# Where expert weights land, where a loop of spare blocks stands, and when two broadcast rows are loaded

## The chip, the cores and the metric

One core of a Trainium2 chip runs the whole program. The metric is the time of one execution in microseconds (us), taken on the device. The core has TensorE (PE), VectorE (DVE), ScalarE (ACT), GpSimd (POOL), and SyncE (SP), which does nothing here but start DMA transfers from its queue, in program order; POOL starts some as well. On-chip tiles lie in SBUF, sums of matmuls in PSUM.

## The reference

The program is two transformer blocks in float32 on 512 tokens of width 1024. Only the end of the second one matters here: a mixture of 32 experts, two for each token.

```python
x = layer_norm_2(alpha * x + (1.0 + gt1) * y, ln_g[l, 0], ln_b[l, 0])
h = x * (1.0 + sc2) + sh2
y = hier_moe(h, w_route_grp[l], w_route_exp[l], w_gate[l], w_up[l], w_down[l])
x = layer_norm_2(alpha * x + (1.0 + gt2) * y, ln_g[l, 1], ln_b[l, 1])
...
# in hier_moe, for the rows xb that were routed to expert e:
hb = jax.nn.silu(xb @ w_gate[e]) * (xb @ w_up[e])
return hb @ w_down[e]
```

Each expert has gate and up weights of 1024 x 512 and down weights of 512 x 1024, 6.29 MB together, 201 MB for all of them.

## The kernel before

The dense part (first block, then the second one's mixer) takes up the first 1520 us or so. After it the pools `pool` (left side of SBUF) and `wpool` (right side) are closed, and `ep1` and `ep2` take over their space; a tile there waits for the old tiles whose bytes it overlaps.

**Weights.** `ew` issues one load of 512 KB from SP's queue into a tile that `eraw` hands out: 128 partitions with 4096 bytes each. `eraw` goes round a ring of 22 such tiles, 12 in `ep1` and 10 in `ep2`. An expert takes twelve loads: four of gate (g), four of up (u), and four of down (d). Each load on SP's queue tells of its landing through one of eight semaphores in turn, and the load eight places further on waits for that one, so no more than eight are under way. In the first pass two loads go into a tile named `first` of the tag `xs` (the list `ex`), as a 23rd and 24th buffer. The program as built puts the `ep1` tiles 480 bytes and the `ep2` tiles 192 bytes past a multiple of 512.

**Compute.** The loop over `e` runs `gate_up` for expert e and, woven into it, `down` for expert e - 1 and one of the eight steps of `gather`, which picks the rows of the next four experts by matmuls with a one-hot matrix (`xg`, line 1751). Each expert has 64 rows. The results `y` go to DRAM (`y_d`) two experts at a time by a store on POOL's queue (line 1884).

**Overflow.** An expert with over 64 rows gets extra blocks. `overflow` runs them in a loop whose count is read from memory (`ovi`) on every engine; with these inputs the body isn't entered, as the trace shows 128 loads of each kind of weight and no more. The loop stands ahead of the expert with index `E_OV` = 8. Just ahead of it `eraw`'s count is set to 0, and the four loads of d of expert 7 and the eight of g and u of expert 8 are issued (`rawd`, `rawg`).

**Residual and last norm.** `residual` starts at index `E_RES` = 14: it loads two broadcast rows (`lg`, `lb`, 512 KB each once spread over partitions) into two tiles of the ring and scales `x_sb` on DVE (8 instructions). At index 28 (`NE - 4`) two more broadcast rows, `lg2` and `lb2`, are loaded into a tile of tag `xs` (lines 1845 and 1846).

**End.** After expert 31's loads, eight indirect loads on POOL's queue (line 1906) fetch each token's two result rows from `y_d` into tiles of the ring. ACT scales the pair of the last token block (line 1935) before POOL adds them (line 1936). A last layer norm follows, and eight stores.

The order of instructions on each engine comes from a scheduler that goes by the program's order and by when buffers come free.

Of the kernel before, what the change touches and what calls it, by code (L numbers as in the profile page):

```python
# [13 lines left out]
F32 = mybir.dt.float32  # L14
# [7 lines left out]
D = 1024  # L22
P = 128
# [26 lines left out]
def tile_model(ctx: ExitStack, tc: tile.TileContext, A: dict, out: bass.AP):  # L50
# [1377 lines left out]
    V.tensor_tensor(hgc, col["ln_g0"], sc2, ALU.mult)  # L1428

    pcol = lambda ap: ap.rearrange("o (q p j) -> p (o q) j", q=4, j=2)  # L1430
    pv = cst(32, "pv").rearrange("p (a q j) -> p a q j", a=4, j=2)
    for i, ap in enumerate((A["ln_g_2"][0, 0:1, :], A["ln_b_2"][0, 0:1, :], mod_row[:, 4 * D : 5 * D], mod_row[:, 3 * D : 4 * D])):
        SY.dma_start(pv[:, i], pcol(ap))
    pv = pv.rearrange("p a q j -> p a (q j)")
# [100 lines left out]
    halve_z(NT - 1)  # L1535

    panels.close()
    ep1 = ctx.enter_context(tc.tile_pool(name="ep1", bufs=1, side="right", reuse_waits="tile"))
    dense.close()
    ep2 = ctx.enter_context(tc.tile_pool(name="ep2", bufs=1, side="left", reuse_waits="tile"))  # L1540
    N1 = NRAW + 8
    N2 = 10
    nraw, ex = [0], []

    def eraw(loop=False):
        i = nraw[0] % (N1 + N2)
        if not loop and ex:
            if nraw[0] >= N1 + N2:
                return ex.pop(0)
        if loop:  # L1550
            i = N1
        else:
            nraw[0] += 1
        if i < N1:
            return ep1.tile([P, D], F32, tag="eraw", name=nm("eraw"), bufs=N1)
        return ep2.tile([P, D], F32, tag="eraw2", name=nm("eraw"), bufs=N2)
# [8 lines left out]
        return raw  # L1565

    wg, wu, wd = A["w_gate_2"][0], A["w_up_2"][0], A["w_down_2"][0]
    raws0 = [ew(w, 2, q) for q in range(4) for w in (wg[0], wu[0])]


    def ytile():
# [5 lines left out]
    def xtile():  # L1577
        return ep2.tile([P, ND * 256], F32, tag="xs", name=nm("xs"), bufs=2)

    first = xtile()  # L1580
    ex.extend(first[:, i * D : (i + 1) * D] for i in range(2))
    xs0 = xtile()
    scr = [etile("scr"), 0]
    oh0 = [ytile(), ytile()]
# [91 lines left out]
    def routing():  # L1676

        ge, gs, e2 = rt(4, "ge"), rt(1, "gs"), rt(1, "e2")
        tc.keep_in_program_order(V.tensor_tensor(ge, gl, bc(gm, 4), ALU.subtract))
        SC.activation(ge, ge, AF.Exp)  # L1680
        tc.keep_in_program_order(V.tensor_tensor(e2, m2, m1, ALU.subtract))
        SC.activation(e2, e2, AF.Exp)
        tc.keep_in_program_order(V.tensor_reduce(gs, ge, axis=AX.X, op=ALU.add))
        V.reciprocal(gs, gs)
        tc.keep_in_program_order(V.tensor_scalar(gate1, e2, 1.0, None, ALU.add))
        V.reciprocal(gate1, gate1)
        V.tensor_tensor(gate1, gate1, gs, ALU.mult)
# [24 lines left out]
        for j in range(2):  # L1712
            V.tensor_tensor(rj[j], rowt, E[j], ALU.mult)
            V.tensor_reduce(rowf[:, j, :], rj[j], axis=AX.X, op=ALU.add)
        V.tensor_copy(rows_i, rowf)

        ovf = cpool.tile([1, 16], F32, name="ovf")
        ovc = rs_(NOV * NE)[0:1].rearrange("p (b e) -> p b e", b=NOV)
        V.tensor_tensor(ovc, oe[0:1, :].rearrange("p (o e) -> p o e", o=1).to_broadcast([1, NOV, NE]),
                        iota[0:1, :NOV].rearrange("p (b o) -> p b o", o=1).to_broadcast([1, NOV, NE]), ALU.is_le)  # L1720
        V.tensor_reduce(ovf[:, 0:NOV], ovc, axis=AX.X, op=ALU.add)
        V.tensor_scalar(ovf[:, 0:NOV], ovf[:, 0:NOV], float(NE - 1), None, ALU.min)
        V.tensor_copy(ovf[:, 15:16], oe[0:1, NE - 1 : NE])
        V.tensor_copy(ovi, ovf)
        V.tensor_scalar(relv, rflat, -float(NE * CAP), None, ALU.add)
# [2 lines left out]
    rowf = cpool.tile([P, 2, NT], F32, name="rowf")  # L1728
    rflat = rowf.rearrange("p j t -> p (j t)")
    rows_i = cpool.tile([P, 2, NT], I32, name="rows_i")  # L1730
    ovi = cpool.tile([1, 16], I32, name="ovi")
    relv = cpool.tile([P, 8], F32, name="relv")

    gt2 = ep2.tile([P, S], F32, name="gt2")
# [22 lines left out]
                V.tensor_scalar(xs[:, c], pv, pg[:, c : c + 1], pb[:, c : c + 1], ALU.mult, ALU.add)  # L1757
            yield

    def gate_up(wg, wu, xs, res, raws=(), loop=False):  # L1760

        ps = mm("gu")
        for q in range(4):
            rw = raws[2 * q : 2 * q + 2] if raws else [ew(w, 2, q, loop) for w in (wg, wu)]
            for k in range(2):
                for m in range(2):
                    PE.matmul(ps[m * CAP : (m + 1) * CAP, :], lhsT=xs[0][:, 2 * q + k, xs[1], :], rhs=rw[m][:, k * S : (k + 1) * S],  # L1767
                              start=q == 0 and k == 0, stop=q == 3 and k == 1)
                if q < 3 or k == 0:
                    yield  # L1770
        g = etile("eg")
        SC.activation(g[CAP:, :], ps[:CAP, :], AF.Silu)  # L1772
        V.tensor_tensor(g[:CAP, :], ps[CAP:, :], g[CAP:, :], ALU.mult)  # L1773
        res.append(g)
        yield

    def down(wd, g, y, raws=(), loop=False, rg=None):

        ps = mm("hT")
        for c in range(4):  # L1780
# [4 lines left out]

        py = acc("py")
        for c in range(4):
            raw = raws[c] if raws else ew(wd, 1, c, loop)
            for half in range(2):
                PE.matmul(py[half * CAP : (half + 1) * CAP, :], lhsT=hT[:, c * CAP : (c + 1) * CAP], rhs=raw[:, half * S : (half + 1) * S],  # L1790
                          start=c == 0, stop=c == 3)
# [13 lines left out]
    def overflow():  # L1805

        n_ov = nc.values_load(ovi[0:1, 15:16], min_val=0, max_val=NOV)
        with tc.For_i(0, n_ov, 1) as ib:
            ei = nc.values_load(ovi[0:1, bass.ds(ib, 1)], engines=(mybir.EngineType.SP,), min_val=0, max_val=NE - 1)
            dyn = lambda w: w[bass.ds(ei, 1)].rearrange("o k n -> (o k) n")  # L1810
            xo, go = [], []
            run(gather(relv, 1, xo))
            run(gate_up(dyn(wg), dyn(wu), (xo[0], 0), go, loop=True))
            yo = ytile()
            run(down(dyn(wd), go[0], yo[:CAP, :], loop=True))
            SY.dma_start(y_d[bass.ds(ib * CAP + NE * CAP, CAP), :], yo[:CAP, :])
            V.tensor_scalar(relv, relv, -float(CAP), None, ALU.add)

    def residual():

        lg, lb = eraw(), eraw()
        SY.dma_start(lg, A["ln_g_2"][0, 0:1, :].partition_broadcast(P))
        SY.dma_start(lb, A["ln_b_2"][0, 0:1, :].partition_broadcast(P))
        for t in range(NT):
# [2 lines left out]
            V.scalar_tensor_tensor(x_sb[t], lb, ALPHA, x_sb[t], ALU.mult, ALU.add)  # L1827
            yield

    E_OV = 8  # L1830
    E_RES = 14
    xg, gx = [], []
    gx.append(gather(None, 4, xg, ov0))
    downs, done = [], []
    for e in range(NE):
# [4 lines left out]
        if e == NE - 4:  # L1840
# [29 lines left out]
        if e == E_OV:  # L1870

            nraw[0] = 0
            rawd = [ew(wd[e - 1], 1, c) for c in range(4)]
            rawg = [ew(w, 2, q) for q in range(4) for w in (wg[e], wu[e])]
            overflow()
            gx.append(gather(rel_cols((e // 4 + 1) * 4 * CAP), 4, xg))
        gu = gate_up(wg[e], wu[e], (xg[e // 4], e % 4), g, rawg)
        for i in range(8):
            next(gu)
            if i == 2 and e:  # L1880
                downs.append(down(wd[e - 1], gp, yp, rawd, rg=rgs[:, 0:1] if e == NE - 1 else None))
            downs = [d for d in downs if next(d, 1) is None]
            if i == 2 and e > 2 and e % 2:
                GP.dma_start(y_d[(e - 3) * CAP : (e - 1) * CAP, :], yd)
# [113 lines left out]
```

## Time and profile before

| what | value |
|---|---|
| time, median of 3 runs | 2114.64 us (2114.31 to 2116.75) |
| the profiled execution's own time | 2116.61 us |
| its span, first to last instruction | 2114.9 us |
| PE busy | 2000.5 us (95%) |
| DVE busy | 1239.6 us (59%) |
| ACT busy | 758.5 us (36%) |
| bytes moved by DMA | 377.05 MB |

Busy time is a share of the whole span, over stages with different limits; a matmul's end is modelled in it, so a busy PE need not be a PE at its peak. The stage of the experts, from about 1520 us on, has to be read from stretches of its own.

### The profile page before, as it was taken

The numbers are of one execution on the slowest core, as the hardware profiler recorded it, in microseconds if no ns is written. First come the engines' busy times: TensorE is split into PE (matmuls) and PEld (weight loads), VectorE is DVE, ScalarE is ACT, GpSimd is POOL, SyncE is SP. The second block draws the span as 40 slices with busy tenths as digits, with TensorE's granted clock in tenths as the row PEclk, the third lists the DMA queues.
The fourth block names the chain that finished last, engine by engine and source line by source line (L and its number), as shares of the span: only waits on it lengthen the run. The fifth ranks groups of instructions, "written<-read, shape, count | busy, mean of one in ns | idle before, by whom it ended". The sixth has DMA issues, their size and how long they took to land. (4 is left out here: it accounts for less than half of the span.)

```text
span 2114.9 us, 25924 instructions
## 1 busy us (share of the span) xinstructions
PE 2000.5 (95%) x9522; PEld 1399.0 (66%) x9522; DVE 1239.6 (59%) x2816; ACT 758.5 (36%) x1403; POOL 91.2 (4%) x117
## 2 busy tenths in 40 slices
PE   7999989999999999999989999999989899999893
PEld 6887668877877778887878877778744343333321
DVE  4898666687468667799998643535542223212216
ACT  4433873443233346754545324542311000000002
POOL 1000100000000010000000000010100000000003
PEclk9999999999999999999999999999989999999997
DMA  4343005366446345533133232143299899999993
GB/s 133 103 105 90 20 21 179 111 203 183 132 149 198 98 119 137 141 78 89 36 79 81 74 89 70 50 120 106 80 352 402 341 409 410 409 410 411 371 411 130
DMA packets 306341, 377.05 MB, mean 178 GB/s; under 512 B 45828, under 2 KB 225548, under 8 KB 306212
## 3 DMA queue, kind: packets, MB, share of 16 engines
q1 hardware_dynamic: 301748, 359.12, 50.7%
q0 software_dynamic: 4464, 16.25, 2.0%
q8 instruction: 76, 1.25, 0.2%
q14 instruction: 53, 0.43, 0.1%
HBM read 354.06 MB, written 21.26 MB: 177 GB/s over the span
## 5 line engine op out<-in xcount | busy, mean ns | idle before, releaser
L99 DVE TENSOR_TENSOR wl<-wraw,wh 128x1024 fp32r<-128x1024 f32 (+1 forms) x196 | 236.8, 1209 | 211.9 <-ACT wh L98 210.8
L98 ACT CAST wh<-wraw 128x1024 fp32r<-128x1024 f32 (+1 forms) x196 | 202.7, 1036 | 398.5 <-PE up L129 72.2
L1767 PE MATMUL gu<-eraw,xs 128*64 128x512 f32 x1016 | 319.8, 616 | 15.4 <-DMA eraw<-in_w_up_dram 8.5
L1767 PEld LDWEIGHTS gu<-eraw,xs 128*64 128x64 f32 x1016 | 82.7, 139 | 155.8 <-issue 102.3
L128 PE MATMUL pc<-hi,wh 128*128 128x512 f32 (+2 forms) x480 | 176.9, 374 | 0.6 <-ACT hi L98 0.4
L129 PE MATMUL pc<-lo,wh 128*128 128x512 f32 (+2 forms) x480 | 173.4, 364 | 0.5 <-DVE lo L99 0.5
L130 PE MATMUL pc<-hi,wl 128*128 128x512 f32 (+2 forms) x480 | 173.1, 363 | 0.0
L1790 PE MATMUL py<-eraw,ehT 128*64 128x512 f32 x512 | 160.5, 603 | 2.8 <-DVE ehT L1783 1.3
L1773 DVE TENSOR_TENSOR eg<-gu,eg 64x512 f32<-64x512 f32 x32 | 22.2, 693 | 236.5 <-ACT eg L1772 236.1
L128 PE MATMUL up<-hi,wh 128*128 128x512 f32 x328 | 130.9, 399 | 0.0
L129 PE MATMUL up<-lo,wh 128*128 128x512 f32 x328 | 129.7, 395 | 0.0
L130 PE MATMUL up<-hi,wl 128*128 128x512 f32 x328 | 129.7, 395 | 0.0
L1772 ACT ACTIVATE eg<-gu 64x512 f32<-64x512 f32 x32 | 18.8, 588 | 283.1 <-PE gu L1767 283.1
L130 PEld LDWEIGHTS pc<-hi,wl 128*128 128x128 f32 (+1 forms) x480 | 90.1, 188 | 12.4
L128 PEld LDWEIGHTS pc<-hi,wh 128*128 128x128 f32 (+1 forms) x480 | 90.0, 189 | 12.5 <-ACT hi L98 1.0
L129 PEld LDWEIGHTS pc<-lo,wh 128*128 128x128 f32 (+1 forms) x480 | 90.5, 189 | 11.4 <-DVE lo L99 0.7
L1790 PEld LDWEIGHTS py<-eraw,ehT 128*64 128x64 f32 x512 | 44.3, 138 | 72.6 <-issue 56.9
L449 DVE SCALAR_TENSOR_TENSOR u<-u,cols_dw 128x497 f32<-128x497 f32 (+14 forms) x120 | 84.8, 750 | 0.7
L1755 ACT ACTIVATE xs<-xg,pb,pg 128x256 f32<-128x256 f32 x32 | 18.0, 564 | 174.1 <-PE xg L1751 174.1
L1751 PEld LDWEIGHTS xg<-oh,zNh 128*128 128x128 f32 x224 | 42.6, 190 | 53.1 <-issue 40.6
L128 PEld LDWEIGHTS up<-hi,wh 128*128 128x128 f32 x328 | 61.6, 188 | 23.8 <-ACT wh L98 7.8
L1757 DVE TENSOR_SCALAR xs<-xg,pg,pb 128x256 f32<-128x256 f32 x32 | 17.4, 543 | 100.4 <-PE xg L1751 100.4
(627 smaller groups left out, 4388.9 us busy)
## 6 DMA issues: line engine op xcount, KB each, us to landing
eraw<-in_w_down_dram SPq DMA_DIRECT2D x128, 512.0 KB
eraw<-in_w_gate_dram SPq DMA_DIRECT2D x127, 512.0 KB
eraw<-in_w_up_dram SPq DMA_DIRECT2D x127, 512.0 KB
wraw<-in_w_in_dram SPq DMA_DIRECT2D x91, 512.0 KB
wada<-in_w_ada_dram SPq DMA_DIRECT2D x48, 512.0 KB
wraw<-in_w_ffn_up_dram SPq DMA_DIRECT2D x44, 512.0 KB
wraw<-in_w_ffn_down_dram SPq DMA_DIRECT2D x20, 512.0 KB
wraw<-in_w_out_dram SPq DMA_DIRECT2D x16, 512.0 KB
```

The costliest lines, as they stand in the source:

```text
L98: c = SC.copy(r(hi), src)
L99: (eng or V).tensor_tensor(r(lo), src, hi, ALU.subtract)
L128: PE.matmul(ps, lhsT=wh, rhs=xh, start=start, stop=False)
L129: PE.matmul(ps, lhsT=wh, rhs=xl, start=False, stop=False)
L130: PE.matmul(ps, lhsT=wl, rhs=xh, start=False, stop=stop)
L449: yield lambda j=j, lo=lo, hi=hi, s=s: V.scalar_tensor_tensor(a[:, lo:hi], u[:, lo + s : hi + s], dww[:, j * 4 + c : j * 4 + c + 1], a[:, ...
L1751: PE.matmul(ps[:, :n], lhsT=hN[t][s_][:, c * P : (c + 1) * P], rhs=r(ov[:, t, :]), start=t == 0 and s_ == 0, stop=t == NT - 1 and s_ == 1)
L1755: SC.activation(xs[:, c], pv, AF.Identity, scale=pg[:, c : c + 1], bias=pb[:, c : c + 1])
L1767: PE.matmul(ps[m * CAP : (m + 1) * CAP, :], lhsT=xs[0][:, 2 * q + k, xs[1], :], rhs=rw[m][:, k * S : (k + 1) * S], start=q == 0 and k == 0 ...
L1772: SC.activation(g[CAP:, :], ps[:CAP, :], AF.Silu)
L1773: V.tensor_tensor(g[:CAP, :], ps[CAP:, :], g[CAP:, :], ALU.mult)
L1790: PE.matmul(py[half * CAP : (half + 1) * CAP, :], lhsT=hT[:, c * CAP : (c + 1) * CAP], rhs=raw[:, half * S : (half + 1) * S], start=c == 0 ...
```

## The change

It does five things. The weight tiles come to lie at multiples of 512 bytes: small tiles (`pv`, `ovf`, `ovi`) leave `cpool`, and paddings of 480 and 64 bytes are put ahead of `ep1` and `ep2`. The `first` tile, and with it the 23rd and 24th buffer, is gone. `overflow` moves from index 8 to 16, with 11 loads issued ahead of it in the order of use and no reset of the ring. `residual` moves from index 14 to 18 and takes tiles of its own (tag `yhl`, which `yh` and `yl` use at the end). `lg2` and `lb2` are loaded at index 30, where they were at 28.

```diff
+    PAD_R = 120
...
-    pv = cst(32, "pv").rearrange("p (a q j) -> p a q j", a=4, j=2)
+    pv = small(32, "pv").rearrange("p (a q j) -> p a q j", a=4, j=2)
...
+    padr = ctx.enter_context(tc.tile_pool(name="padr", bufs=1, side="right"))
+    GP.memset(padr.tile([P, PAD_R], F32, name="padr"), 0.0)
     ep1 = ctx.enter_context(tc.tile_pool(name="ep1", bufs=1, side="right", reuse_waits="tile"))
     dense.close()
+    padl = ctx.enter_context(tc.tile_pool(name="padl", bufs=1, side="left"))
     ep2 = ctx.enter_context(tc.tile_pool(name="ep2", bufs=1, side="left", reuse_waits="tile"))
...
     def eraw(loop=False):
+        if loop:
+            return ep2.tile([P, D], F32, tag="yhl", name=nm("lraw"), bufs=2)
         i = nraw[0] % (N1 + N2)
-        if not loop and ex:
-            if nraw[0] >= N1 + N2:
-                return ex.pop(0)
-        if loop:
-            i = N1
-        else:
-            nraw[0] += 1
+        nraw[0] += 1
...
-    raws0 = [ew(w, 2, q) for q in range(4) for w in (wg[0], wu[0])]
+    early = {}
+
+    def ld(w, e, q):
+
+        if (w, e, q) in early:
+            return early.pop((w, e, q))
+        return ew({"g": wg, "u": wu, "d": wd}[w][e], 1 if w == "d" else 2, q)
+
+    def ahead(e, n):
+
+        for i in range(n):
+            x = "g0 u0 g1 u1 d0 g2 u2 d1 d2 g3 u3 d3".split()[i % 12]
+            k = (x[0], e + i // 12 - (x[0] == "d"), int(x[1]))
+            if k[1] >= 0:
+                early[k] = ld(*k)
+
+    ahead(0, 12)
...
-    first = xtile()
-    ex.extend(first[:, i * D : (i + 1) * D] for i in range(2))
...
-        ovf = cpool.tile([1, 16], F32, name="ovf")
+        ovf = small(16, "ovf")[0:1, :]
...
-    ovi = cpool.tile([1, 16], I32, name="ovi")
+    ovi = padl.tile([P, 16], I32, name="ovi")[0:1, :]
...
-        lg, lb = eraw(), eraw()
+        lg, lb = eraw(True), eraw(True)
...
-    E_OV = 8
-    E_RES = 14
+    E_OV = 16
+    E_RES = 18
...
-            SY.dma_start(lg2, A["ln_g_2"][0, 1:2, :].partition_broadcast(P))
-            SY.dma_start(lb2, A["ln_b_2"][0, 1:2, :].partition_broadcast(P))
...
+        if e == NE - 2:
+            SY.dma_start(lg2, A["ln_g_2"][0, 1:2, :].partition_broadcast(P))
+            SY.dma_start(lb2, A["ln_b_2"][0, 1:2, :].partition_broadcast(P))
...
         if e == E_OV:
-
-            nraw[0] = 0
-            rawd = [ew(wd[e - 1], 1, c) for c in range(4)]
-            rawg = [ew(w, 2, q) for q in range(4) for w in (wg[e], wu[e])]
+            ahead(e, 11)
             overflow()
...
-    yh = ep2.tile([P, D], F32, name="yh")
-    yl = ep2.tile([P, D], F32, name="yl")
+    yh, yl = (ep2.tile([P, D], F32, tag="yhl", name=nm("yhl"), bufs=2) for _ in range(2))
```

Three places in the order of instructions follow. The first is SP's queue just ahead of the loop, which begins with the load of `ovi`. Before, the first of these rows is the last of four loads of expert 7's down weights, and the rest are expert 8's gate and up weights:

```order
L1564 DMA eraw_14007<-in_w_down_dram 128x1024
L1562 DMA eraw_14009<-in_w_gate_dram 128x1024
L1562 DMA eraw_14011<-in_w_up_dram 128x1024
L1562 DMA eraw_14013<-in_w_gate_dram 128x1024
L1562 DMA eraw_14015<-in_w_up_dram 128x1024
L1562 DMA eraw_14017<-in_w_gate_dram 128x1024
L1562 DMA eraw_14019<-in_w_up_dram 128x1024
L1562 DMA eraw_14021<-in_w_gate_dram 128x1024
L1562 DMA eraw_14023<-in_w_up_dram 128x1024
L1807 TENSOR_LOAD ovi
L1808 COMPARE_AND_BRANCH
```

In the changed kernel the eleven rows ahead of the loop are loads of experts 15 (down) and 16 (gate, up):

```order
L1563 DMA eraw_14706<-in_w_gate_dram 128x1024
L1563 DMA eraw_14708<-in_w_up_dram 128x1024
L1563 DMA eraw_14710<-in_w_gate_dram 128x1024
L1563 DMA eraw_14712<-in_w_up_dram 128x1024
L1565 DMA eraw_14714<-in_w_down_dram 128x1024
L1563 DMA eraw_14716<-in_w_gate_dram 128x1024
L1563 DMA eraw_14718<-in_w_up_dram 128x1024
L1565 DMA eraw_14720<-in_w_down_dram 128x1024
L1565 DMA eraw_14722<-in_w_down_dram 128x1024
L1563 DMA eraw_14724<-in_w_gate_dram 128x1024
L1563 DMA eraw_14726<-in_w_up_dram 128x1024
L1822 TENSOR_LOAD ovi
```

The loop went from between experts 7 and 8 to between 15 and 16, and one load fewer stands ahead of it.

The second place is where the two broadcast rows stand on SP's queue, before between loads of expert 28:

```order
L1564 DMA eraw_15936<-in_w_down_dram 128x1024
L1562 DMA eraw_16002<-in_w_gate_dram 128x1024
L1845 DMA xs_15948<-in_ln_g_dram 128x1024
L1846 DMA xs_15948<-in_ln_b_dram 128x1024
L1562 DMA eraw_16004<-in_w_up_dram 128x1024
L1562 DMA eraw_16010<-in_w_gate_dram 128x1024
```

In the changed kernel they stand ahead of expert 30's loads:

```order
L1565 DMA eraw_16122<-in_w_down_dram 128x1024
L1875 DMA xs_15957<-in_ln_g_dram 128x1024
L1876 DMA xs_15957<-in_ln_b_dram 128x1024
L1563 DMA eraw_16137<-in_w_gate_dram 128x1024
L1563 DMA eraw_16139<-in_w_up_dram 128x1024
L1563 DMA eraw_16145<-in_w_gate_dram 128x1024
```

They moved behind some two experts' worth of weight loads.

The third is POOL's queue at the end, from the last store of results to the last indirect load. Before, two indirect loads of token block 2, two of block 3, the additions of block 3, and then blocks 0 and 1:

```order
L1884 DMA y_d<-ey_15947 128x1024
L1906 DMA eraw_16268<-y_d,rows_i 128x1024
L1906 DMA eraw_16270<-y_d,rows_i 128x1024
L1906 DMA eraw_16272<-y_d,rows_i 128x1024
L1906 DMA eraw_16274<-y_d,rows_i 128x1024
L1936 TENSOR_TENSOR eraw_16272<-eraw_16272,x_12644 128x1024
L1936 TENSOR_TENSOR x_12644<-eraw_16274,eraw_16272 128x1024
L1906 DMA eraw_16260<-y_d,rows_i 128x1024
```

In the changed kernel (block 3's tiles are `eraw_16281` and `eraw_16283`):

```order
L1896 DMA y_d<-ey_15956 128x1024
L1919 DMA eraw_16273<-y_d,rows_i 128x1024
L1919 DMA eraw_16275<-y_d,rows_i 128x1024
L1919 DMA eraw_16277<-y_d,rows_i 128x1024
L1919 DMA eraw_16279<-y_d,rows_i 128x1024
L1919 DMA eraw_16281<-y_d,rows_i 128x1024
L1919 DMA eraw_16283<-y_d,rows_i 128x1024
L1948 TENSOR_TENSOR eraw_16281<-eraw_16281,x_12644 128x1024
L1948 TENSOR_TENSOR x_12644<-eraw_16283,eraw_16281 128x1024
```

Block 1's pair now stands ahead of block 3's, since other tiles of the ring come free first.

## Rows read from the trace of the kernel before

**Rows 1.** The page: what the DMA engines moved, in 40 equal slices.

```profile
GB/s 133 103 105 90 20 21 179 111 203 183 132 149 198 98 119 137 141 78 89 36 79 81 74 89 70 50 120 106 80 352 402 341 409 410 409 410 411 371 411 130
```

**Rows 2.** Stretches of 20 us: engines' busy time, clock, DMA share, GB/s.

```profile
1560.00:1580.00 20.00, 20.00 (x99) 7.90 (x99) 4.85 (x15) 3.02 (x4) 0.00 (x0) 1.00 0.86 323
...
1660.00:1680.00 20.00, 14.68 (x62) 5.74 (x62) 7.27 (x17) 0.59 (x1) 0.53 (x1) 0.89 0.67 241
...
1760.00:1780.00 20.00, 20.00 (x93) 7.79 (x94) 8.78 (x17) 1.15 (x2) 0.00 (x0) 1.00 1.03 409
1780.00:1800.00 20.00, 15.66 (x67) 4.97 (x64) 9.32 (x11) 1.18 (x2) 0.53 (x1) 0.91 1.03 411
...
1980.00:2000.00 20.00, 14.26 (x80) 5.11 (x77) 5.75 (x17) 0.59 (x1) 0.00 (x0) 0.91 0.82 307
```

**Rows 3.** Waits of SP's queue, 1690 to 1960 us: us in total, times, longest.

```profile
SPq L1562 <- DMA eraw<-in_w_up_dram: 46.9, 49, 2.9
...
SPq L1562 <- PE gu L1767: 2.4, 10, 0.4
```

**Rows 4.** Timeline around the loop: start us, us, engine, line, operation, tile.

```profile
1659.69 0.33 SPq L1562 DMA_DIRECT2D eraw<-in_w_up_dram  x1
...
1670.28 0.33 SPq L1562 DMA_DIRECT2D eraw<-in_w_gate_dram  x1
...
1671.14 0.33 SPq L1562 DMA_DIRECT2D eraw<-in_w_up_dram  x1
...
1676.22 1.98 PE L1767 MATMUL gu<-eraw,xs 128*64 128x512 f32 x4 [5.12 <-SPq L1808]
...
1677.44 0.34 SPq L1562 DMA_DIRECT2D eraw<-in_w_gate_dram  x1
```

**Rows 5.** The instructions of line 1845: duration ns min/median/max, first and last start.

```profile
L1845 SPq EVENT_SEMAPHORE  x2: 17/4783/9549, 1979.4 to 1980.3; - x2
```

**Rows 6.** Timeline of ACT: the Silu that ends experts 6, 7, and 19 to 23.

```profile
1658.83 0.59 ACT L1772 ACTIVATE eg<-gu 64x512 f32<-64x512 f32 x1 [9.45 <-PE gu L1767]
1670.28 0.59 ACT L1772 ACTIVATE eg<-gu 64x512 f32<-64x512 f32 x1 [10.86 <-PE gu L1767]
...
1860.87 0.59 ACT L1772 ACTIVATE eg<-gu 64x512 f32<-64x512 f32 x1 [12.30 <-PE gu L1767]
...
1878.26 0.59 ACT L1772 ACTIVATE eg<-gu 64x512 f32<-64x512 f32 x1 [4.77 <-PE gu L1767]
...
1910.68 0.59 ACT L1772 ACTIVATE eg<-gu 64x512 f32<-64x512 f32 x1 [9.45 <-PE gu L1767]
...
1925.34 0.59 ACT L1772 ACTIVATE eg<-gu 64x512 f32<-64x512 f32 x1 [14.07 <-PE gu L1767]
```

**Rows 7.** Timeline of SP: issue of the last up load of expert 6, of 20.

```profile
1630.13 0.33 SPq L1562 DMA_DIRECT2D eraw<-in_w_up_dram  x1
...
1864.04 0.33 SPq L1562 DMA_DIRECT2D eraw<-in_w_up_dram  x1
```

**Rows 8.** Timeline of SP: the 24th load of weights and the 25th.

```profile
1547.32 0.33 SPq L1562 DMA_DIRECT2D xs<-in_w_up_dram  x1
...
1556.75 0.33 SPq L1564 DMA_DIRECT2D eraw<-in_w_down_dram  x1
```

**Rows 9.** DMA packets of 1700 to 1760 us, and of 1376 to 1377 us.

```profile
DMA packets 6768, 24.64 MB, mean 411 GB/s; under 512 B 761, under 2 KB 761, under 8 KB 6764
...
DMA packets 680, 0.35 MB, mean 348 GB/s; under 512 B 1, under 2 KB 680, under 8 KB 680
```

**Rows 10.** The end: two rows of ACT's timeline, then one of the chain, then ACT's.

```profile
2068.52 1.15 ACT L1935 ACTIVATE eraw<-eraw,r_gate 128x1024 f32<-128x1024 f32 x1 [23.34 <-DMA eraw<-y_d,rows_i]
...
2070.68 1.15 ACT L1935 ACTIVATE eraw<-eraw,r_gate 128x1024 f32<-128x1024 f32 x1 [1.01 <-DMA eraw<-y_d,rows_i]
...
2059.92 10.69 DMA eraw<-y_d,rows_i
...
2071.86 0.59 ACT L1772 ACTIVATE eg<-gu 64x512 f32<-64x512 f32 x1
```

More of the change, by code (lines that the diff above doesn't have):

```diff
@@ L1542, in tile_model @@
     N2 = 10
-    nraw, ex = [0], []
+    nraw = [0]
     def eraw(loop=False):
+        if loop:
+            return ep2.tile([P, D], F32, tag="yhl", name=nm("lraw"), bufs=2)
         i = nraw[0] % (N1 + N2)
-        if not loop and ex:
-            if nraw[0] >= N1 + N2:
-                return ex.pop(0)
-        if loop:
-            i = N1
-        else:
-            nraw[0] += 1
+        nraw[0] += 1
         if i < N1:
@@ L1758, in gather, with gate_up @@
             yield
-    def gate_up(wg, wu, xs, res, raws=(), loop=False):
+    def gate_up(load, xs, res):
         ps = mm("gu")
         for q in range(4):
-            rw = raws[2 * q : 2 * q + 2] if raws else [ew(w, 2, q, loop) for w in (wg, wu)]
+            rw = [load(w, q) for w in "gu"]
             for k in range(2):
@@ L1775, in gate_up, with down @@
         yield
-    def down(wd, g, y, raws=(), loop=False, rg=None):
+    def down(load, g, y, rg=None):
         ps = mm("hT")
@@ L1787, in down @@
         for c in range(4):
-            raw = raws[c] if raws else ew(wd, 1, c, loop)
+            raw = load("d", c)
             for half in range(2):
@@ L1809, in overflow @@
             ei = nc.values_load(ovi[0:1, bass.ds(ib, 1)], engines=(mybir.EngineType.SP,), min_val=0, max_val=NE - 1)
-            dyn = lambda w: w[bass.ds(ei, 1)].rearrange("o k n -> (o k) n")
+            dyn = lambda w, q: ew({"g": wg, "u": wu, "d": wd}[w][bass.ds(ei, 1)].rearrange("o k n -> (o k) n"), 1 if w == "d" else 2, q, loop=True)
             xo, go = [], []
             run(gather(relv, 1, xo))
-            run(gate_up(dyn(wg), dyn(wu), (xo[0], 0), go, loop=True))
+            run(gate_up(dyn, (xo[0], 0), go))
             yo = ytile()
-            run(down(dyn(wd), go[0], yo[:CAP, :], loop=True))
+            run(down(dyn, go[0], yo[:CAP, :]))
             SY.dma_start(y_d[bass.ds(ib * CAP + NE * CAP, CAP), :], yo[:CAP, :])
@@ L1863, in tile_model @@
         g = []
-        rawg, rawd = (), ()
         if e == 0:
-            rawg = raws0
             routing()
@@ L1870, in tile_model @@
         if e == E_OV:
-            nraw[0] = 0
-            rawd = [ew(wd[e - 1], 1, c) for c in range(4)]
-            rawg = [ew(w, 2, q) for q in range(4) for w in (wg[e], wu[e])]
+            ahead(e, 11)
             overflow()
             gx.append(gather(rel_cols((e // 4 + 1) * 4 * CAP), 4, xg))
-        gu = gate_up(wg[e], wu[e], (xg[e // 4], e % 4), g, rawg)
+        load = lambda w, q, e=e: ld(w, e, q)
+        gu = gate_up(load, (xg[e // 4], e % 4), g)
         for i in range(8):
@@ L1880, in tile_model @@
             if i == 2 and e:
-                downs.append(down(wd[e - 1], gp, yp, rawd, rg=rgs[:, 0:1] if e == NE - 1 else None))
+                downs.append(down(loadp, gp, yp, rg=rgs[:, 0:1] if e == NE - 1 else None))
             downs = [d for d in downs if next(d, 1) is None]
@@ L1893, in tile_model @@
                 next(gx[-1], None)
-        gp, yp = g[0], y[e % 2 * CAP : (e % 2 + 1) * CAP, :]
+        gp, loadp, yp = g[0], load, y[e % 2 * CAP : (e % 2 + 1) * CAP, :]
         if e % 2:
@@ L1898, in tile_model @@
         run(d)
-    rawsd = [ew(wd[NE - 1], 1, c) for c in range(4)]
+    for c in range(4):
+        early["d", NE - 1, c] = ld("d", NE - 1, c)
     yas = []
@@ L1907, in tile_model @@
             yas.append(ya)
-    run(down(wd[NE - 1], gp, yp, rawsd, rg=rgs[:, 1:2]))
-    yh = ep2.tile([P, D], F32, name="yh")
-    yl = ep2.tile([P, D], F32, name="yl")
+    run(down(loadp, gp, yp, rg=rgs[:, 1:2]))
+    yh, yl = (ep2.tile([P, D], F32, tag="yhl", name=nm("yhl"), bufs=2) for _ in range(2))
     for p0 in (0, CAP):
```

## Prediction

> **What bounds the kernel now.** I read the page's slices first. DMA moves 409 to 411 GB/s in most slices from the thirtieth on and falls short in a few [rows 1]. Stretches of 20 us show where: 323 GB/s as the experts start, 241 at the loop, 307 after 1980 us, and 409 to 411 elsewhere [rows 2]. Against 411, they lose 20 x (1 - 323/411) = 4.3 us, 8.3 us and 5.1 us of transfer time.
>
> PE looks full in the same stretches, so the next view is what SP's queue waits for. From 1690 to 1960 us it is the landing of earlier loads (the first of several such rows has 46.9 us in 49 waits), and hardly ever PE's freeing of a buffer (2.4 us) [rows 3]. So the stream of weights is the bound there, and a microsecond in which it runs dry is lost unless the ring was full anyway. One load takes 512 KB / 411 GB/s = 1.28 us.
>
> How near is PE? Experts 20 to 23 end 64.47 us after expert 19 (1860.87 to 1925.34), which is 1.34 us for each of 48 loads, stores of results included [rows 6]. The three that carry steps of the one-hot matmuls take 49.81 us together (to 1910.68). An expert without such steps and with its weights there took 11.45 us (expert 7). So PE alone would need 61.3 us for four. It has 5% to spare: a gain of the stream up to that is not taken back by PE.
>
> The stock of weights matters for the loop. Expert 6's last up load was issued 28.7 us before its Silu, some 21 loads ahead in a ring of 22; expert 20's 14.2 us before, 10.6 loads [rows 6, 7]. So the ring is full until the loop, the loop uses the stock up, and from then on PE takes weights as they come.
>
> **The loop.** Before, SP issues a load at 1659.69 us and the next two only at 1670.28 and 1671.14, since the reset ring makes them wait for buffers of expert 7; then the loop holds it until 1677.44, while PE idles 5.12 us [rows 4]. That is the 8.3 us. Now eleven loads in ring order stand ahead of the loop. What stock will there be at expert 15's end? From 21 at expert 6, expert 7 uses 12 loads in 11.45 us, in which 11.45/1.34 = 8.5 arrive: 17.5. Each four experts then use up (64.5 - 61.3)/1.34 = 2.4 more, which leaves 12.7 after two rounds. When SP has issued the eleventh load, PE is 1.7 loads (2.3 us) short of the loop. From PE's end (1676.22 - 5.12 = 1671.1) to SP's next issue at 1677.44 it took 6.3 us. That makes 8.6 us, and the eight loads under way last 8 x 1.28 = 10.2. So the stream hardly runs dry; I leave 1.0 us for the restart, and the term is a gain of 7.3 us. Bounds: nothing lost (8.3), or a ring still full, where PE is eleven loads away and the stream is dry for 14.7 + 6.3 + 1 - 10.2 = 11.8 us (3.5 us worse than now).
>
> **The two rows of the last norm.** Their tile was last read by expert 27's matmuls, so SP stood 9.5 us at line 1845 with all weights queued behind it [rows 5], and the stream lost 5.1 us. At index 30 that tile has been free for two experts. The bytes stay; broadcasts of the same size in the middle of the stream (the residual's, issued at 1759 us) left 409 GB/s around them [rows 2]. Gain 5.1 us; bound below 3.4, should the slow 2 us after the wait be the broadcast's own.
>
> **The start.** Two buffers fewer. SP issued the 24th load at 1547.32 us and the 25th at 1556.75, when PE freed the first tile [rows 8]; now the 23rd waits for that, up to 2 x 1.28 = 2.6 us of transfer lost. But the ring is still full at expert 6 [rows 6, 7], so until then the stream waits for PE now and then, and catches up most of it. I take a loss of 1.0 (0 to 2.6). The paddings make the first tiles overlap two old ones each, and a load may start some microseconds later; the wait at the 23rd load hides it. Without that cover it costs up to 5 us. `pv`'s four loads now stand between `x_sb`'s, but what they feed comes only with the first expert; behind the memset of the padding POOL has only `gt2`, which the first `down` needs. Nothing for both.
>
> **Residual.** Its eight DVE instructions made PE idle 20 - 15.66 = 4.3 us in one stretch, and the stream went on at 411 GB/s [rows 2]. At index 18 it follows soon after the loop's pause: a stock of 12.7 loads grows by some 5 there, some 2 with the next three experts, and 3 here, to about the 22 of the ring. A loss of 1.0 us (0 to 4). The two ring tiles it no longer takes gain nothing while the ring isn't full.
>
> **The end.** ACT scales the last block's pair as it lands, at 2068.52 and 2070.68 us, and expert 31's Silu stands behind that at 2071.86; the chain runs through this landing (10.69 us) [rows 10]. Two more indirect loads now stand ahead of that pair: 2 x 1.28 = 2.6 us later for all that follows. Bounds 0 and 4.3, twice the 2.16 us between the two landings.
>
> **Alignment.** No row has a large aligned transfer to SBUF, so I bound it. Packets of 512 bytes, at 480 past a multiple of 512, go at 680 x 512 bytes in 1 us, 23.5 ns for each of 16 engines; weights at 4096 bytes and 411 GB/s take 159.5 [rows 9]. A line through both has 37.9 ns per 1024 bytes and 4.1 ns per packet. A surcharge for an unaligned start can't be over these 4.1 ns, so alignment gives between nothing and 2.6% of some 354 loads (384 less those ahead of PE's start): 354 x 1.28 x 0.026 = 11.6 us. I take nothing: if an extra block of 256 bytes were moved for each packet, the short ones would take 19 + 9.5 = 28.5 ns, far from 23.5.
>
> The Trainium skill (DMA: Bandwidth & Descriptors, "How a descriptor splits into AXI transactions") says that a descriptor which doesn't start on a 256-byte boundary begins its first transaction at the boundary below and pays for the bytes before its start. For a 4096-byte row that is up to 7 beats on 128, so by the page alone the loads would gain some 5%, an estimate of 24 us, and the sum below would be 31.8 instead of 7.8. The 348 GB/s of the short packets speak against it, and no run here shows an aligned row.
>
> **Sum.** 7.3 + 5.1 - 1.0 - 1.0 - 2.6 = 7.8 us gained. The profiled execution took 2116.61 us with its span of 2114.9, so it would take 2108.8; it stands 2.0 us above the median of 2114.64, on which the forecast is 2106.8 us.
>
> **Rivals.**
>
> Alignment counts. By the bound above 11.6 us come on top, with PE's 5% just enough for it: 2106.8 - 11.6 = 2095.2. For it speaks that every weight tile is unaligned today and that 411 GB/s is so steady; against it the short packets. Chance 0.2.
>
> The pause only moves, or PE binds. If PE's 5.12 us of idleness and not the dry stream is what the loop costs, moving it gains nothing: 5.1 - 1.0 - 1.0 - 2.6 = 0.5, or 2114.1. For it speaks that PE is busy for 20.00 of 20 us at 1760 us [rows 2]; against it SP's waits [rows 3]. Chance 0.17.
>
> Slower: the ring is still full at expert 16. Then the stream runs dry for 11.8 us against 8.3, and the sum is -3.5 + 5.1 - 1.0 - 1.0 - 2.6 = -3.0: 2117.6. It decides from a stock of 15 loads on (3.3 x 1.34 = 4.4 us more than forecast, half the term), and above 20 the change loses. For it speaks the 21 at expert 6, against it PE's faster pace. Chance 0.08.
>
> **Numbers.** The forecast has 0.55, between 2102 and 2111. Below 2092 lies some 0.1 (alignment at its full bound together with other gains), above 2113 some 0.1, so the range is 2092 to 2113. Faster or slower by 0.2%, 4.2 us, is about what a measurement can tell. Under 2110.4 lie all of the alignment's 0.2, 0.52 of the forecast and 0.03 of the others: 0.75. Above 2118.9 lies half of the slower rival and a little for the unseen: 0.06. The rest is 0.19.
>
> **What would show it.** The stretch at 1660 us should be at 400 GB/s or more, the new place of the loop (near 1800 us) should lose under 3 us, and the one after 1980 us should be full. SP should not wait at line 1875. ACT should scale the last pair some 13 us, not 10.7, after its issue. Stretches in mid-stream should stay at 409 to 412 GB/s; 420 or more would mean that alignment counts and that I am wrong by some ten microseconds. A stretch at the loop under 250 GB/s would bear out the slower rival.

## The result, and the profile after

The changed kernel takes 2102.61 us (median of 4 runs, 2098.05 to 2102.82) against 2115.07 for the kernel before (4 runs, 2114.31 to 2116.75): a ratio of 0.9934, with a 95% interval of 0.9919 to 0.9949. It is 12.5 us faster; 7.8 were forecast. The profiled execution took 2102.81 us with a span of 2101.1.

The page shows the first surprise. This is its row of GB/s in 40 slices, the answer to [rows 1]:

```profile
GB/s 131 107 105 91 21 21 171 110 200 186 145 131 193 114 104 143 158 74 81 45 89 72 73 91 71 60 109 92 49 320 419 408 419 419 371 420 419 419 419 107
```

Where [rows 1] had 409 to 411 there is 419 to 420 now, in the middle of the stream, in slices in which neither the loop nor the broadcast rows stood before or stand now. The same stretches of 20 us as in [rows 2], in the changed kernel (start:end, length, busy time of PE, weight loads, DVE, ACT, POOL, then granted clock, DMA share, GB/s):

```profile
1660.00:1680.00 20.00, 20.00 (x94) 7.82 (x90) 3.85 (x7) 1.15 (x2) 0.53 (x1) 1.00 1.02 405
...
1740.00:1760.00 20.00, 20.00 (x92) 8.27 (x92) 3.49 (x6) 1.71 (x3) 0.53 (x1) 1.00 1.03 419
1780.00:1800.00 20.00, 14.13 (x60) 5.28 (x58) 6.72 (x16) 0.59 (x1) 0.53 (x1) 0.83 0.77 310
1800.00:1820.00 20.00, 20.00 (x104) 8.25 (x104) 4.01 (x7) 1.71 (x3) 0.53 (x1) 1.00 1.02 404
...
1980.00:2000.00 20.00, 19.22 (x110) 6.94 (x111) 7.79 (x21) 0.59 (x1) 0.53 (x1) 1.00 1.03 419
```

Three things are read here. The old place of the loop (1660) is full but for 14 GB/s (SP waits there for buffers that PE still reads), and the old place of the two broadcast rows (1980) is full. The new place of the loop loses 20 x (1 - 310/420) + 20 x (1 - 404/420) = 6.0 us, where 1.0 was forecast and 8.3 were lost before. And everything between runs at 419 to 420.

The loop itself in steps of 1 us, same columns:

```profile
1792.00:1793.00 1.00, 0.00 (x0) 0.00 (x0) 0.42 (x1) 0.00 (x0) 0.00 (x0) 0.95 1.03 422
1793.00:1794.00 1.00, 0.00 (x0) 0.00 (x0) 0.00 (x0) 0.00 (x0) 0.00 (x0) 0.50 0.80 320
1794.00:1795.00 1.00, 0.00 (x0) 0.00 (x0) 0.00 (x0) 0.00 (x0) 0.00 (x0) 0.50 0.24 98
1795.00:1796.00 1.00, 0.00 (x0) 0.00 (x0) 0.00 (x0) 0.00 (x0) 0.00 (x0) 0.50 0.02 8
1796.00:1797.00 1.00, 0.60 (x2) 0.29 (x4) 0.68 (x3) 0.00 (x0) 0.00 (x0) 0.50 0.00 0
1797.00:1798.00 1.00, 1.00 (x4) 0.00 (x0) 1.00 (x4) 0.00 (x0) 0.00 (x0) 0.50 0.02 8
1798.00:1799.00 1.00, 1.00 (x5) 0.70 (x4) 1.00 (x4) 0.00 (x0) 0.00 (x0) 0.50 0.13 45
1799.00:1800.00 1.00, 1.00 (x7) 0.94 (x6) 0.57 (x3) 0.00 (x0) 0.00 (x0) 0.63 0.77 246
```

DVE, the last engine at work, is done by 1792.5, but nothing starts. The traffic of the loads under way runs out at 1795; DVE and PE start again at 1796.3 and 1796.4, and the next load's bytes flow from 1799 on. SP's timeline and its waits (us in total, times, longest) fit to it:

```profile
1784.51 0.33 SPq L1563 DMA_DIRECT2D eraw<-in_w_up_dram  x1
1797.67 0.34 SPq L1565 DMA_DIRECT2D eraw<-in_w_down_dram  x1
...
SPq L1823 <- SPq L1823: 9.8, 6, 3.6
```

Within line 1823, the loop's head, SP stands 9.8 us in six pieces. So the forecast's picture, in which the loop's 6.3 us pass while eight loads are still landing, isn't what the rows show. They look as if the loop first let all eight land.

The end, as POOL and ACT see it (the answer to [rows 10]):

```profile
2039.00 1.04 POOL L1919 DMA_INDIRECT eraw<-y_d,rows_i  x1 [7.84 <-DMA eraw<-in_w_gate_dram]
...
2044.09 0.93 POOL L1919 DMA_INDIRECT eraw<-y_d,rows_i  x1 [0.30 <-PE gu L1782]
2045.33 0.94 POOL L1919 DMA_INDIRECT eraw<-y_d,rows_i  x1 [0.30 <-issue]
2055.56 2.35 POOL L1948 TENSOR_TENSOR eraw<-eraw,x 128x1024 f32<-128x1024 f32 x1 [9.30 <-ACT eraw L1947]
...
2060.55 1.23 POOL L1919 DMA_INDIRECT eraw<-y_d,rows_i  x1
...
2054.33 2.38 ACT L1947 ACTIVATE eraw<-eraw,r_gate 128x1024 f32<-128x1024 f32 x2 [26.15 <-DMA eraw<-y_d,rows_i]
2056.73 0.59 ACT L1787 ACTIVATE eg<-gu 64x512 f32<-64x512 f32 x1
```

Expert 31's Silu (L1787) starts right behind ACT's two scales, which wait for the fifth and the sixth indirect load.

**How the runs are compared.** Up to the first weight load all kernels run the same instructions on PE, ACT and POOL (in the kernel before, `pv`'s loads stand elsewhere, and some others move with them), but the profiled executions came to it at 1488.32 to 1494.85 us. So beside the medians I use the time from the first weight load to the end of the span: 2114.9 - 1494.85 = 620.1 us before, 2101.1 - 1493.99 = 607.1 after. That column is one execution each. All ratios are to the kernel before on the same chip.

| kernel | median us | ratio (95%) | first load to end us |
|---|---|---|---|
| before | 2115.07 | 1 | 620.1 |
| changed | 2102.61 | 0.9934 (0.9919 to 0.9949) | 607.1 |
| tiles shifted back | 2108.54 | 0.9973 (0.9963 to 0.9982) | 616.5 |
| before, aligned only | 2105.33 | 0.9957 (0.9944 to 0.9971) | 614.4 |
| tiles at 256 | 2098.89 | 0.9933 (0.9919 to 0.9947) | 606.1 |
| tiles at 64 | 2110.89 | 0.9983 (0.9974 to 0.9992) | 615.7 |
| tiles at 32 | 2109.43 | 0.9974 (0.9963 to 0.9986) | 615.5 |
| sixteen ahead | 2101.08 | 0.9937 (0.9924 to 0.9951) | 606.2 |
| none ahead | 2108.81 | 0.9970 (0.9958 to 0.9982) | 612.1 |
| loop at 8 | 2102.35 | 0.9941 (0.9927 to 0.9954) | 608.0 |
| no loop | 2095.77 | 0.9909 (0.9896 to 0.9923) | 604.4 |
| rows at 28 | 2105.95 | 0.9958 (0.9944 to 0.9971) | 610.4 |
| Silu ahead of scales, loads in order | 2093.30 | 0.9895 (0.9879 to 0.9910) | 599.6 |
| Silu ahead of scales alone | 2098.51 | 0.9924 (0.9911 to 0.9938) | 604.8 |

### The profile page after: what moved, and what is told of

Its sections match the earlier page's. It is cut to its first block, busy times and chain, and to the rows that moved or that the text cites. A ratio compares the mean times of both kernels' runs of the same rounds, so it can differ in the third digit from the quotient of the medians.

```text
span 2101.1 us, 25962 instructions
## 1 busy us (share of the span) xinstructions
PE 1992.3 (95%) x9522; PEld 1398.9 (67%) x9522; DVE 1239.9 (59%) x2816; ACT 758.2 (36%) x1403; POOL 91.3 (4%) x118
## 3 DMA queue, kind: packets, MB, share of 16 engines
q8 instruction: 76, 1.25, 0.2%
## 5 line engine op out<-in xcount | busy, mean ns | idle before, releaser
L99 ACT CAST wh<-wraw 128x1024 fp32r<-128x1024 f32 (+1 forms) x196 | 202.7, 1037 | 396.1 <-PE up L130 71.6
L1782 PE MATMUL gu<-eraw,xs 128*64 128x512 f32 x1024 | 321.0, 610 | 12.7 <-SPq L1823 5.9
L1805 PE MATMUL py<-eraw,ehT 128*64 128x512 f32 x512 | 166.7, 608 | 1.4 <-DVE ehT L1798 1.3
L1787 ACT ACTIVATE eg<-gu 64x512 f32<-64x512 f32 x32 | 18.8, 588 | 269.9 <-PE gu L1782 269.9
L131 PEld LDWEIGHTS pc<-hi,wl 128*128 128x128 f32 (+1 forms) x480 | 90.1, 188 | 12.3
L1766 PEld LDWEIGHTS xg<-oh,zNh 128*128 128x128 f32 x224 | 42.5, 190 | 53.1 <-issue 38.9
```

The costliest lines, as they stand in the source:

```text
L99: c = SC.copy(r(hi), src)
L131: PE.matmul(ps, lhsT=wl, rhs=xh, start=False, stop=stop)
L1766: PE.matmul(ps[:, :n], lhsT=hN[t][s_][:, c * P : (c + 1) * P], rhs=r(ov[:, t, :]), start=t == 0 and s_ == 0, stop=t == NT - 1 and s_ == 1)
```

## The experiments

**Is it the tiles' place?** The theory is that the multiple of 512 bytes gives the 2%; the rival is that the new order of the loads does. One kernel takes the place alone away, the other gives it alone to the kernel before.

```diff
-    padr = ctx.enter_context(tc.tile_pool(name="padr", bufs=1, side="right"))
-    GP.memset(padr.tile([P, PAD_R], F32, name="padr"), 0.0)
...
-    ovi = padl.tile([P, 16], I32, name="ovi")[0:1, :]
+    ovi = padl.tile([P, 64], I32, name="ovi")[0:1, :16]
```

> The changed kernel with its weight tiles back where they were before, 480 and 192 bytes past a multiple of 512; loop, rows and end stay as changed. Theory: the place of a tile sets the pace of the stream, so mid-stream stretches fall from 419-420 to 409-411 GB/s, and some 354 loads at 1.25 us lose 2%: about 9 us, 2111.5 (2109 to 2113). Rival: the faster stream comes from the other edits (ring order of the loads, broadcasts elsewhere): 2102.5 and still 419.

It took 2108.54 us, a little under the range expected, and from the first load on 9.4 us more than the changed kernel. The same stretch in mid-stream as above, here:

```profile
1740.00:1760.00 20.00, 20.00 (x91) 7.99 (x87) 4.83 (x8) 1.74 (x3) 0.53 (x1) 1.00 1.03 411
```

PE is as busy as ever; only the bytes are fewer. Then the kernel before with `pv`, `ovf`, `ovi` and the two paddings as in the changed one, and nothing else of the change:

> The kernel before with the two paddings alone, so that its weight tiles begin at multiples of 512 bytes; loop, rows and end as before. Theory: mid-stream at 419 instead of 409-411 GB/s and about 9 us less, some 2106 (2104 to 2109), the three gaps of the stream unchanged. Rival: 2115 and 411 GB/s.

It took 2105.33 us, with 419 in mid-stream and the gaps at the loop and at the broadcast rows still there:

```profile
1740.00:1760.00 20.00, 20.00 (x93) 8.26 (x93) 3.49 (x6) 1.72 (x3) 0.53 (x1) 1.00 1.03 419
1660.00:1680.00 20.00, 13.96 (x54) 5.24 (x52) 5.32 (x13) 1.15 (x2) 0.00 (x0) 0.75 0.64 230
1980.00:2000.00 20.00, 16.95 (x88) 6.29 (x85) 5.75 (x17) 0.59 (x1) 0.00 (x0) 0.83 0.86 342
```

Both ways the place of the tiles is worth 8 to 9 us by the ratios (0.9973 - 0.9934 = 0.0039, and 1 - 0.9957 = 0.0043, of 2115 us). From the first load on it is 9.4 us one way and 620.1 - 614.4 = 5.7 the other, where 1.3 us went ahead of the first expert: its Silu came 72.9 us after the first load, and 71.6 in the kernel before. The rival is out.

**How fine must the place be?** Three kernels with all 22 tiles at 256, 64 and 32 bytes past a multiple of 512, by the sizes of the two paddings alone:

```diff
-    PAD_R = 120
+    PAD_R = 56
...
-    ovi = padl.tile([P, 16], I32, name="ovi")[0:1, :]
+    ovi = padl.tile([P, 80], I32, name="ovi")[0:1, :16]
```

(104 and 32 for the place at 64, 112 and 24 for that at 32.)

> The changed kernel with all its weight tiles 256 bytes past a multiple of 512. If a boundary of 256 bytes or less is what counts, 419 GB/s and 2102.5, as with 512. If 512 is needed, 411 GB/s and 2111.5.

> The changed kernel with all its weight tiles 64 bytes past a multiple of 512. If 64 bytes are enough, the stream keeps 419 GB/s, and the 10 of 22 tiles that stood at 192 before were never a burden: 2100 (2098 to 2103). If 256 are needed, 410 GB/s and 2108.5, as with the tiles where they were.

> The changed kernel with all its weight tiles 32 bytes past a multiple of 512. If 64 bytes are what counts, this is at 410 GB/s or below and at 2108.5 or above, since now all 22 tiles are off and not 12 of them: up to 2110. If 32 are enough, 419 GB/s and 2100.

256 is as good as 512; 64 and 32 are as bad as the old places. The DMA packets of 1700 to 1760 us, in the answer to [rows 9], first of the kernel with tiles at 256:

```profile
DMA packets 6902, 25.16 MB, mean 419 GB/s; under 512 B 767, under 2 KB 767, under 8 KB 6899
```

and of the one with tiles at 32:

```profile
DMA packets 6747, 24.60 MB, mean 410 GB/s; under 512 B 750, under 2 KB 750, under 8 KB 6744
```

So the boundary that counts lies above 64 and at most at 256 bytes (128 was not tried), and being off it costs the same at 32 as at 64 or at the old mix of 480 and 192.

**What does the loop cost?** At first the theory was still the forecast's: the stock of loads decides, it was only larger than I had worked out, so more loads must stand ahead.

```diff
-            ahead(e, 11)
+            ahead(e, 16)
```

> The changed kernel with 16 loads issued ahead of the loop instead of 11. Theory: SP stands 13.2 us at the loop because the stock of loads is 16 to 18, five to seven more than it puts ahead; with 16 ahead it reaches the loop when PE does, stands some 6 us, and the eight loads under way cover that. The stretch at the loop stays at 410 or more, and the 6 us of transfer lost there come back: about 2097 (2096 to 2099). Rival: what the loop costs is PE's own idle time of 5.9 us, which no load ahead removes: 2102.5.

That theory fell: 606.2 us from the first load on against 607.1, and a loss of the same size, only later. The timeline of that kernel around the loop:

```profile
1791.96 0.33 SPq L1563 DMA_DIRECT2D eraw<-in_w_up_dram  x1
1802.82 0.62 DVE L1673 TENSOR_SCALAR oh<-iota,rel 128x256 f32<-128x256 f32 x2 [10.98 <-SPq L1823]
...
1802.92 1.98 PE L1782 MATMUL gu<-eraw,xs 128*64 128x512 f32 x4 [12.98 <-SPq L1823]
...
1803.74 0.34 SPq L1565 DMA_DIRECT2D eraw<-in_w_down_dram  x1
```

Now PE and DVE stand 11 to 13 us and SP is the one that all wait for. SP's last load went out at 1791.96; eight loads at 1.25 us are 10.0 us, and PE goes on 10.96 us after it. In the changed kernel the same distance is 1796.40 - 1784.51 = 11.9 us, although there PE had ended its work some 6 us before it went on. This is the new theory: SP leaves the loop only when all that it has under way has landed, so a dry stretch of some 5.5 us (about 2 to leave, the rest until bytes flow again) belongs to the loop wherever it stands and however many loads stand ahead. Three kernels test it. The loop at its old place:

```diff
-    E_OV = 16
+    E_OV = 8
```

> The changed kernel with the loop back ahead of expert 9, eleven loads still ahead of it. Theory, after the run with 16 loads ahead: SP enters the loop only when all loads under way have landed and PE has come, so a dry stretch of some 5.5 us belongs to the loop wherever it stands. With a full ring PE is eleven loads away when SP arrives, 14 us against 10 for the loads to land: 4 us more, a loss of 9 to 10 in the stretch, of which a full ring gives some back: 2104 to 2107. Rival: it makes no difference where the loop stands: 2102.5.

```profile
1660.00:1680.00 20.00, 17.19 (x69) 6.47 (x66) 5.74 (x14) 1.15 (x2) 0.00 (x0) 0.83 0.78 299
1680.00:1700.00 20.00, 20.00 (x105) 8.44 (x106) 3.58 (x6) 1.71 (x3) 0.53 (x1) 1.00 1.01 406
```

These are the stretches of its loop: 5.7 + 0.6 = 6.3 us lost, and 2102.35 us in all. The place makes no difference that the intervals show. The 4 us that I added for a full ring did not come: PE ended its work at 1667.2, 9.4 us after SP's last load at 1657.78 and a microsecond after the traffic, not 14 us after it. Next, no loop (`overflow()` not called):

> The changed kernel without the loop of extra row blocks, which is left out altogether (with these inputs its body is never entered); the eleven loads are still issued together. If the drained queue is what the loop costs, its 6.0 us of transfer come back: 2096.5 (2095 to 2098), no stretch under 400 between 1680 and 2040 us. Rival: PE is too near to its own limit to use them: 2101.

2095.77 us, and the stretches at 1780 and 1800 us are at 421 and 417 GB/s. By the medians 6.8 us come back, by the ratios 5.3 (0.0025 x 2115), and in the one profiled execution, the longest of its five, 2.7 from the first load on. In that execution the first expert's Silu came 72.9 us after the first load, in the changed kernel's 71.4, so from there on it is 4.2; what is left of the difference to 6.0 stays open. Then no load ahead (`ahead(e, 0)`):

> The changed kernel with no load ahead of the loop at its new place. SP comes to the loop some 17 loads before PE, 22 us; the loads under way last 10, so the stream is dry for 12 us more than the drain itself takes: 2114 (2111 to 2116), a stretch at the loop with 17 us missing. If only the drain counts and not what stands ahead of it: 2102.5.

```profile
1780.00:1800.00 20.00, 16.46 (x66) 5.77 (x60) 6.09 (x15) 0.98 (x2) 0.53 (x1) 0.83 0.49 188
...
SPq L1823 <- DVEq L1822: 6.5, 1, 6.5
```

This stretch loses 11.0 us, the next 0.5, which is 5.5 more than with eleven ahead; the kernel is 6.2 us slower by the median. I had expected 11.5: PE ended its work 16.9 us after SP's last load (1789.87 - 1772.96), not 22, and 6 us after the traffic had ended. The second row is SP's wait at the loop's head for DVE, which itself had waited for PE; no such row of that length stands in the changed kernel's trace. So a dry stretch is the longer of two waits, for the engines' work and for the landings. Eleven loads ahead take away the first; sixteen did not take away the second.

**The two rows of the last norm,** back at index 28:

> The changed kernel with the loads of the two rows of the last norm back at index 28. Theory: SP stands some 9 us behind expert 27, the stretch after 1980 us falls to about 310 GB/s, and it takes 5.1 us more: 2107.6. Rival: the faster stream has stock enough by then, or the experts behind it make it up: 2102.5.

SP stands there again, now 10.3 us, and two stretches fall short (398 and 370 GB/s, 1.0 + 2.3 us):

```profile
SPq L1860 <- PE gu L1782: 10.3, 1, 10.3
...
1960.00:1980.00 20.00, 19.14 (x87) 6.28 (x84) 3.30 (x7) 0.73 (x2) 0.53 (x1) 1.00 0.98 398
1980.00:2000.00 20.00, 17.10 (x88) 6.59 (x87) 5.75 (x17) 0.45 (x1) 0.00 (x0) 0.83 0.93 370
```

The cost is 3.3 us by the medians and from the first load on, 5.1 by the ratios (0.0024 x 2115), whose intervals overlap a little; one stretch at 310 GB/s was expected.

**The end.** PE has ended expert 31's gate and up at 2043.8 us in the changed kernel, 13 us before the Silu (the 2044.6 of the expectation is the end of expert 30's down). If that Silu waits only for the two scales, it must come forward when they stand behind it. One kernel traces the scales after the Silu and keeps the indirect loads in the order of their blocks, too; the other leaves out the second edit:

```diff
-            GP.indirect_dma_start(out=ya, out_offset=None, in_=y_d, in_offset=bass.IndirectOffsetOnAxis(ap=rows_i[:, j, t : t + 1], axis=0))
+            tc.keep_in_program_order(GP.indirect_dma_start(out=ya, out_offset=None, in_=y_d, in_offset=bass.IndirectOffsetOnAxis(ap=rows_i[:, j, t : t + 1], axis=0)))
...
+    for ya, gate in zip(yas[6:8], (gate1, gate2)):
+        tc.keep_in_program_order(SC.activation(ya, ya, AF.Copy, scale=gate[:, 3, :]))
     run(down(loadp, gp, yp, rg=rgs[:, 1:2]))
...
-            SC.activation(rows, rows, AF.Copy, scale=gate)
```

> The changed kernel with the eight indirect loads in the order of their blocks on POOL and ACT's two scales behind expert 31's Silu and the casts. Theory: PE has ended expert 31's gate and up at 2044.6 us, and its Silu, at 2056.73, waits for nothing but the two scales ahead of it; with Silu at some 2045 all that follows moves ahead by about 10 us, to 2092 (2089 to 2096). Rival: the last indirect loads and what waits for them set the end, and 2 to 4 us are left: 2100.

> The changed kernel with ACT's two scales behind expert 31's Silu, and the indirect loads in the order that they had. Theory: Silu at 2045 as in the run with both edits, but the first block's pair is still issued only after POOL's two sums, at some 2060 us, and lands at 2070, so that half of the gain is left: 2098 (2096 to 2100). Rival: the order of the indirect loads counts for nothing: 2093.

ACT with both edits:

```profile
2045.37 0.59 ACT L1787 ACTIVATE eg<-gu 64x512 f32<-64x512 f32 x1 [15.63 <-PE gu L1782]
...
2058.35 2.36 ACT L1922 ACTIVATE eraw<-eraw,r_gate 128x1024 f32<-128x1024 f32 x2 [0.77 <-DMA eraw<-y_d,rows_i]
```

The Silu waits for PE now and starts 11.4 us earlier, and the kernel takes 2093.30 us: 9.3 less by the medians, 8.2 by the ratios, 7.5 from the first load on. It is the fastest kernel here that leaves nothing out. With the scales alone moved it is 2098.51 (4.1, 2.1 and 2.3 us): the Silu starts at 2044.70, but POOL issues the last two indirect loads only behind its two sums, at 2062.64 and 2064.17 us. These two us aren't clear of the noise (the intervals of the ratios overlap); the 8.2 of both edits are.

## Why the prediction was right, and where it was wrong

The sign and the range were right; that the size came out near was luck in part, for two errors partly cancel: alignment gave 9.5 us where nothing was put down, and the loop 5.0 less than its term. In stretches of the profile, the parts are: alignment +9.5, loop +2.3, rows +5.1, start -1.3, residual 0, end -3.3; together 12.3. The list leaves out the stretches in which the full ring holds SP (1620 to 1660 us before, 1.8 us; 1640 to 1680 after, 1.3), so a sum near the measured 12.5 is no proof of each part.

**The bound.** The stream of weights bounds the experts: less lost transfer came out as less time, with PE's 5% enough for it, but only just. The Silu that ends experts 7, 11, 19, 23 and 27 in the changed kernel:

```profile
1669.10 0.59 ACT L1787 ACTIVATE eg<-gu 64x512 f32<-64x512 f32 x1 [10.86 <-PE gu L1782]
...
1729.39 0.59 ACT L1787 ACTIVATE eg<-gu 64x512 f32<-64x512 f32 x1 [10.86 <-PE gu L1782]
...
1855.93 0.59 ACT L1787 ACTIVATE eg<-gu 64x512 f32<-64x512 f32 x1 [14.15 <-PE gu L1782]
...
1916.46 0.59 ACT L1787 ACTIVATE eg<-gu 64x512 f32<-64x512 f32 x1 [11.11 <-PE gu L1782]
...
1978.90 0.59 ACT L1787 ACTIVATE eg<-gu 64x512 f32<-64x512 f32 x1 [12.17 <-PE gu L1782]
```

With a stock of loads PE takes 60.3 us for four experts (61.3 were put down), and 60.5 from expert 19 to 23. Only from 23 to 27 does it go at the stream's pace, 62.4 us. So PE has some 3% left against the faster stream, and a further gain of the stream would soon be lost to PE's own pace.

**Alignment: the step that failed** is "I take nothing". The bound was sound: 4.1 ns of 159.5 per packet at most, 2.6%; the runs show 410 to 411 against 419 to 420 GB/s, 2.0 to 2.2%, or 354 x 1.28 x 0.021 = 9.5 us, and the ratios 8 to 9. What failed was the choice inside the bound. I ruled out a surcharge of a whole block of 9.5 ns and took that for ruling out any; the real one is some 3.3 ns (2.1% of 159.5), which the short packets of [rows 9] allow. (The line through both rows has 38.9 ns per 1024 bytes, not 37.9, and a block would be 9.7; neither changes the bound.) "420 or more would mean that alignment counts and that I am wrong by some ten microseconds" was the right sign to name. The Trainium skill (DMA: Bandwidth & Descriptors, "How a descriptor splits into AXI transactions") puts the boundary at 256 bytes. On that the runs agree with it as far as they go: 256 is free, 64 and 32 are not. They don't agree with its price, which grows with the bytes between the boundary and the start: by the page, an estimate, 1 beat (its unit of transfer) on 128 at 32 bytes past it (0.8%) and 7 at 224 (5.5%), where the runs show 2% at every place off it that was tried.

**The loop: a term mis-sized, by a wrong picture.** 7.3 us were forecast, 2.3 came by the stretches (8.3 - 6.0). The step that failed is "the eight loads under way last 8 x 1.28 = 10.2. So the stream hardly runs dry". I took the 6.3 us between PE's end and SP's next issue in [rows 4] as the loop's own time, running beside the loads. But there only two loads were under way, issued at 1670.28 and 1671.14, and they were landing in those 6.3 us. With eight under way SP stands 13.2 us. The stock was misjudged too (16 to 18 loads rather than 12.7), but the kernel with 16 ahead shows that this did not matter. That SP waits for the landings stands in the changed kernel's trace itself: at line 1823 SP's queue has a wait for each of the eight semaphores by which its loads tell of their landing. Five of them end at 1789.45, 1790.70, 1791.95, 1793.21 and 1794.50 us, one load's time apart, and that of the load issued last at 1795.68; the other engines wait behind them, and PE goes on at 1796.40. A loop that does not wait was not tried.

**The rows of the last norm.** Forecast 5.1, bound below 3.4; the stretch is full as foreseen, and SP stands 0.8 us at line 1875. Taken back, they cost 3.3 to 5.1.

**The start** is as forecast in kind: the 23rd load waits for PE from 1543.28 to 1555.75 us, and the three stretches from 1520 us on move 944 instead of 972 GB/s (281, 368 and 323 before; 312, 307 and 325 now), 1.3 us. Little or nothing of it is left later: expert 7's Silu comes 175.4 us after the first load before and 175.1 now, and SP waits for PE to free buffers again at 1640 us, so the ring is full by then. **The residual** cost nothing, where 1.0 was put down: 419 and 420 GB/s at 1820 and 1840 us.

**The end.** Right in kind and a little small: from the first indirect load to the end it takes 2101.1 - 2039.00 = 62.1 us, before 2114.9 - 2056.07 = 58.8, so 3.3 for 2.6. "Some 13 us, not 10.7, after its issue" was put wrongly: the pair still lands 10 us after its issue, but is itself issued 2.5 us later behind the first indirect load. That the Silu behind it carries the end, which the forecast said of [rows 10], is shown by the two last kernels.

**The rivals.** "Alignment counts" is what happened; its 2095.2 was too low since the loop gave 5 us less than the sum it was put on. "The pause only moves" is half true: at either place the loop costs its 6 us, but PE does not bind yet, and what stands ahead of the loop gave 2 us back. The slower rival had the right place with the wrong rule: the wait for PE is real (5.5 us with none ahead), but a full ring at expert 9 added none of it. (By the forecast's own stock of 12.7, the 3.3 loads from which it was to decide lead to a stock of 16, not 15; SP came to the loop with 18.)

## What to carry to other kernels

Where a stream of loads is the bound, put its buffers on multiples of 256 bytes and look at GB/s in a stretch without gaps: 2% of a rate shows there most plainly. Before you count loads under way as cover for a wait, see in a trace whether the wait is for those very loads; a loop in the program was, here, and cost 6 us with an empty body. At the end of a kernel, read each engine's queue for what stands ahead of the instruction that everything waits for; moving two scales behind it, and two loads forward, was worth 7.5 to 9.3 us, well over half of what the whole change gave.

## What the runs showed of the hardware

Weight loads of 512 KB in packets of 4096 bytes run at 419 to 420 GB/s into tiles at 0 or 256 bytes past a multiple of 512, and at 408 to 412 into tiles at 32, 64 or a mix of 192 and 480 past it, in the stretches without gaps of all the kernels here. And kernels that run the same instructions in the same order up to the first weight load (all but the kernel before and the one without the loop) came to it at 1488.32 to 1494.27 us, 6.0 us apart, half of what the whole change is worth.
